# Twelve of sixteen tiles of h from seven half-size products, in two rounds that share their sums of a

## The chip, the cores and the metric

The kernel runs on one core of one Trainium2 chip. The metric is the device time of one execution in microseconds. A profile of one execution comes with it; its span, from the first to the last instruction, is somewhat shorter than the device time of the same run.

## The reference

```python
m, k, n, p = 1024, 1024, 2048, 1024
h = np.matmul(a, b)                     # a: 1024 x 1024, b: 1024 x 2048
h = 0.5 * h * (1 + np.tanh(np.sqrt(2 / np.pi) * (h + 0.044715 * h ** 3)))
return np.matmul(h, c).astype(np.float32)   # c: 2048 x 1024
```

All inputs and the output are float32 in HBM.

## The kernel before

The kernel computes h transposed. `hT[h]` holds, for one half h (0 or 1) of the 1024 rows of a, sixteen tiles t of 128 columns of h by 512 rows. A tile is a sum over eight k of a product of a 128x128 block of b (the stationary operand) with a 128x512 block of `aT`, the transposed a in bf16. A matmul of 512 columns is the unit of work on TensorE.

*Loads.* SyncE loads a and b in float32 into staging tiles, in pieces of 512 KB: four pieces of a (each one half h and 256 columns of k, a quarter q) and four of b (two k by 512 columns). VectorE or ScalarE casts them to bf16 (`cast_a`, `cast_b`). POOL issues the loads that cast on the way: the rest of a (`a2`), of b (`b1` for its first 1024 columns, `b2` for the others) and all of c (`c_sb`). They wait behind `gate`, a copy of one element on POOL that waits for SyncE's fifth piece. So SyncE's pieces have the DMA engines to themselves at first.

*Turns.* `turn1` and `turn` transpose eight 128x128 blocks of a on TensorE into PSUM; VectorE copies them to `aT`.

*The plain part.* Tiles 0 to 3 of both halves are accumulated over k 0 to 3 as the pieces arrive (`block`, `mm1`), and leave PSUM as float32 (`leave`, tile `half`). Tiles 4 to 7 follow over all eight k. Then tiles 0 to 3 get k 4 to 7 and are added to `half`. `gelu` on ScalarE writes `hT`. That is 128 matmuls (line L112).

*The rounds of seven products.* Tiles 8 to 15 come from a 2x2 block scheme with seven products in place of eight (class `Seven`, function `seven`). In order of issue `seven` calls them P1 (A11 B11), P2 (A12 B21), P5 (S1 T1), P6 (S2 T2), P7 (S3 T3), P3 (S4 B22) and P4 (-A22 T4). A is the quarter of b or of h, B that of a or of c. S1 to S4 and T1 to T4 are sums of quarters that VectorE forms in fp32r (`s1` to `s4`, `t1` to `t4`, line L199). `plain_s` and `plain_t` are ScalarE copies of A22 (negated) and of B22 into the same type. P1 and P2 read bf16, the other five fp32r. Product j of each kind makes one 128x512 tile; its matmuls are at line L241. P1, P6, P7 and P4 accumulate in the banks X (0 to 3), P2, P5 and P3 use the banks Y (4 to 7). After P1, P6 and P7 ScalarE takes snapshots of a bank (`snap`: p1, v and u, line L286). VectorE adds them to the Y banks (`plus`, line L291, tile `ot` with four buffers). Here `done` is `gelu` on the result. The object `one` makes tiles 8 to 15 this way (112 matmuls, k = 4 per product), and `two` the whole second product, h times c, into the output (216 matmuls of 512 columns and 16 of 256). The function `between` places the sums of a round, and the first sums of the next, between its products.

Each engine runs its instructions in the order in which the program writes them (`manual_schedule`). Where `seven` gives the end of a round, two of its parts that matter below are:

```python
        for j in range(4):
            done(1, 1, j, c22[j])
            w.product(py[j], w.last_s, w.t[3], j, False)
            done(0, 1, j, plus(py[j], v[j]))
        between("P3")
```

and, in `between1`, the sums of the second round t1, s1 and t2, in four pieces each, that VectorE forms from there on.

The large SBUF slots x0 to x3, a, b1 and b2 are used by one tile after the other: staging first, then `half` and the sums. A new tile in a slot waits for the last reader of the old one.

Of the kernel before, what the change touches and what calls it, by code (L numbers as in the profile page):

```python
# [19 lines left out]
def kernel(ctx, tc, a, b, c, out):  # L20
# [43 lines left out]
    stb = slot("x0", [128, 2, KH, H], F32, "stb")  # L64
    sta = slot("x1", [128, 2, 2, 4, 256], F32, "sta")

    def load_a(h, q):
        nc.sync.dma_start(out=sta[:, h, q], in_=av[:, 4 * h:4 * h + 4, ds(q * 256, 256)])  # L68

    def load_b(q, c):  # L70
        nc.sync.dma_start(out=stb[:, c, 2 * q:2 * q + 2], in_=bv[:, 2 * q:2 * q + 2, ts(c, H)])  # L71

    load_a(0, 0)
    load_b(0, 0)
    load_a(1, 0)
    load_a(0, 1)
    load_b(1, 0)
    load_a(1, 1)
    load_b(0, 1)
    load_b(1, 1)  # L80

    nc.gpsimd.tensor_copy(gate, stb[:, 0, 3, 0:1])
# [6 lines left out]
    a2 = {}  # L89
    for h in (0, 1):  # L90
        for m in (0, 2):
            st = pieces("m", 4, [128, 2, H], BF16, "a2")
            nc.gpsimd.dma_start(out=st, in_=av[:, 4 * h + m:4 * h + m + 2, ds(KH * 128, H)])
            a2[h, m] = st
    for k in range(KH, KT):
        nc.gpsimd.dma_start(out=b1[:, k], in_=bv[:, k, 0:1024])
# [13 lines left out]
    def mm1(p, t, h, ks, k0=0, k1=KT):  # L110
        for k in ks:
            nc.tensor.matmul(p, b1[:, k, ts(t, 128)], aT[:, h, k],  # L112
                             start=(k == k0), stop=(k == k1 - 1))
# [12 lines left out]
    def cast_a(h, q, eng):  # L126
        ab = pieces("ab", 2, [128, 4, 256], BF16, "ab")
        copy(eng, ab, sta[:, h, q])
        return ab

    def turn1(h, q, i, ab):
# [6 lines left out]
    def cast_b(k, c, n=1):  # L138
        for i in range(n):
            r = ds(i * (H // n), H // n)  # L140
            nc.scalar.activation(b1[:, k, ds(c * H + i * (H // n), H // n)], stb[:, c, k, r], AF.Copy)  # L141

    def block(h, tiles, ks):
        for k in ks:
            for t in tiles:
                mm1(ps[h, t], t, h, (k,), 0, KH)

    stir(7)
    turn1(0, 0, 4, cast_a(0, 0, nc.vector))
    stir(8)  # L150
    cast_b(0, 0, 2)
    cast_b(1, 0)
    block(0, range(4), (0, 1))
    turn1(1, 0, 5, cast_a(1, 0, nc.vector))
    for t in range(3):
        ps[1, t] = bank(4 + t)
    ab = cast_a(0, 1, nc.scalar)
    block(1, range(3), (0,))
    turn1(0, 1, 7, ab)
    block(1, range(3), (1,))  # L160
    cast_b(2, 0)
    cast_b(3, 0)
    ab = cast_a(1, 1, nc.vector)
    block(0, range(4), (2,))
    turn1(1, 1, 7, ab)
    block(0, range(4), (3,))
    for k in range(KH):
        cast_b(k, 1)
    half = slot("x3", [128, 2, 4, H], F32, "half")

    def leave(h, t):
        copy(nc.vector if t % 2 else nc.scalar, half[:, h, t], ps[h, t])


    for t in range(4):
        leave(0, t)
    block(1, range(3), (2, 3))
    ps[1, 3] = bank(7)
    mm1(ps[1, 3], 3, 1, range(KH), 0, KH)
    for t in range(4):  # L180
        leave(1, t)

    def turn(h, m, i):
        pt = bank(i, (128, KH, 256), BF16, "pt")
        for k in range(KH):
            for n in range(2):
                nc.tensor.transpose(pt[:, k, ts(n, 128)], a2[h, m][:, n, ts(k, 128)], ident)  # L187
        nc.vector.tensor_copy(aT[:, h, KH:KT, ds(m * 128, 256)], pt)


    class Seven:
        def __init__(self, kt, A, B, s, t):
            self.kt, self.A, self.B, self.s, self.t = kt, A, B, s, t
# [7 lines left out]
        def t1(self, n=1):  # L201
            self.dve(self.t[0], self.B[0][1], self.B[0][0], SUB, n)

        def t2(self, n=1):
            self.dve(self.t[1], self.B[1][1], self.t[0], SUB, n)

        def t3(self, n=1):
            self.dve(self.t[2], self.B[1][1], self.B[0][1], SUB, n)
# [18 lines left out]
        def plain_t(self, n=1):  # L227
            w = self.kt // n
            for i in range(n):
# [3 lines left out]
        def plain_s(self, n=1):  # L233
            w = self.kt // n
            for i in range(n):
# [3 lines left out]
        def product(self, p, l, r, j, start, c0=0, w=H):  # L239
            for k in range(self.kt):  # L240
# [4 lines left out]
    x = [slot(f"x{i}", [128, 2, 4, H], F32R, "x1") for i in range(3)]  # L245
    one = Seven(4, [[b2[:, 0:4, 0:H], b2[:, 4:8, 0:H]], [b2[:, 0:4, H:], b2[:, 4:8, H:]]],
                [[aT[:, 0, 0:4], aT[:, 1, 0:4]], [aT[:, 0, 4:8], aT[:, 1, 4:8]]],
                [x[i][:, 0] for i in range(3)] + [None], [x[i][:, 1] for i in range(3)] + [None])
    one.t1()


    T2 = [(h, t) for h in range(2) for t in range(4, 8)]
    for n, (h, t) in enumerate(T2[:7]):
        ps[h, t] = bank(n)
        mm1(ps[h, t], t, h, range(KH))
        if n in (2, 3, 4, 5):
            turn(n // 4, 2 * (n % 2), 7)
    one.t3()
    one.t2()
    for k in range(KH, KT):  # L260
        for h, t in T2[:4]:
            mm1(ps[h, t], t, h, (k,))
    for n, (h, t) in enumerate(T2[:7]):
        if n >= 4:
            mm1(ps[h, t], t, h, range(KH, KT))
# [171 lines left out]
```

## Time and profile before

| | |
|---|---|
| device time, three runs | 120.61, 120.62, 120.70 us |
| device time of the profiled run | 120.74 us |
| span of the profile | 119.0 us |
| TensorE, matmuls | 111.3 us busy, 94% |
| TensorE, weight loads | 72.6 us busy, 61% |
| VectorE | 88.5 us busy, 74% |
| ScalarE | 52.7 us busy, 44% |
| POOL | 14.6 us busy, 12% |
| granted TensorE clock | 1.0 |
| read from HBM, written | 20.97 MB, 4.19 MB |

By stage, from the busy times of each engine in each stretch:

| stretch, us | what | TensorE | VectorE | ScalarE |
|---|---|---|---|---|
| 0 to 14.2 | SyncE's loads, first blocks | 10.58 | 4.43 | 5.07 |
| 14.2 to 39.84 | plain part | 25.48 | 17.46 | 12.12 |
| 39.84 to 64.91 | first round (`one`) | 25.07 | 22.07 | 19.61 |
| 64.91 to 115.3 | second round (`two`) | 50.21 | 44.16 | 15.89 |

In the profile PE is TensorE's matmuls, PEld its weight loads, DVE is VectorE, ACT is ScalarE, POOL is GpSimd and SP is SyncE; SPq and POOLq are their issues of DMAs. A line such as "L241 PE MATMUL ps<-x,s ... x48" is a group of 48 matmuls from line 241 that read tiles x and s and write tile ps. In brackets stands the idle time ahead of an instruction and what ended it. Matmuls overlap in time, so the duration of one is longer than the distance between two starts.

### The profile page before, as it was taken

What the parts mean: (1) busy time and instruction counts of PE and PEld (TensorE: products, weight loads), DVE (VectorE), ACT (ScalarE), POOL (GpSimd) and SP (SyncE); (2) the same over time, 40 slices, a digit from 0 to 9 for tenths busy, and PEclk for the clock granted to TensorE, in tenths of its full rate; (3) what the DMA queues carried; (4) which work ended last, traced back from release to release, by engine and by line L of the source; (5) the groups of instructions that cost most, each with busy time, mean ns of one, the idle gap of its engine ahead of it and who ended that gap; (6) DMA issues with size and microseconds to landing.
All of it is one profiled execution on the core that took longest, in us unless ns stands there. A gap on an engine that the chain in (4) does not pass through costs nothing.

```text
span 119.0 us, 1467 instructions
## 1 busy us (share of the span) xinstructions
PE 111.3 (94%) x552; PEld 72.6 (61%) x558; DVE 88.5 (74%) x93; ACT 52.7 (44%) x86; POOL 14.6 (12%) x27
## 2 busy tenths in 40 slices
PE   5877999999999999999999999999999999999970
PEld 2424445554444445888887444488888888888850
DVE  0242689579048899797779999999999986944760
ACT  4045492005647789846679347800043982000000
POOL 2002985453222000000000000000000000000000
PEclk9999999999999999999999999999999999999999
DMA  2999999999999999995000000070000002024992
GB/s 89 280 364 374 347 204 212 170 206 205 207 209 211 213 211 210 212 211 107 4 3 0 6 0 0 0 264 0 0 0 0 6 0 88 0 90 178 357 354 79
DMA packets 11606, 16.86 MB, mean 142 GB/s; under 512 B 720, under 2 KB 6096, under 8 KB 11600
## 3 DMA queue, kind: packets, MB, share of 16 engines
q0 software_dynamic: 5952, 8.39, 39.9%
q1 hardware_dynamic: 5648, 8.39, 20.1%
q8 instruction: 4, 0.07, 0.2%
q14 instruction: 2, 0.02, 0.0%
HBM read 20.97 MB, written 4.19 MB: 212 GB/s over the span
## 4 chain that ended last, share of the span: by engine, by line
PE 85%; DMA 8%; SPq 2%; DVE 1%; issue 1%; DVEq 0%
PE ps L241 63%; PE ps L112 20%; DMA sta<-in_a_dram 8%; PE pt L187 2%; SPq L68 1%; SPq L71 1%; DVE ab L108 1%; PE pt L135 1%; DVE ot L342 0%; DVEq L108 0%
## 5 line engine op out<-in xcount | busy, mean ns | idle before, releaser
L112 PE MATMUL ps<-aT,b 128*128 128x512 bf16 x124 | 28.8, 379 | 2.0 <-ACT b L141 0.9
L241 PE MATMUL ps<-x,s 128*128 128x512 f32 x128 | 29.5, 390 | 0.0
L241 PEld LDWEIGHTS ps<-x,s 128*128 128x128 f32 x128 | 24.0, 188 | 5.1 <-DVE ot L291 0.2
L112 PEld LDWEIGHTS <-b 128*128 128x128 bf16 x128 | 12.1, 98 | 15.6 <-ACT b L141 1.5
L241 PE MATMUL ps<-x,x 128*128 128x512 f32 x64 | 14.8, 389 | 0.0
L241 PE MATMUL ps<-c_sb,hT 128*128 128x512 bf16 (+1 forms) x70 | 14.1, 355 | 0.1
L241 PEld LDWEIGHTS ps<-x,x 128*128 128x128 f32 x64 | 12.0, 188 | 2.5
L286 ACT ACTIVATE v<-ps 128x512 f32<-128x512 f32 x8 | 4.8, 599 | 15.4 <-PE ps L241 15.4
L241 PE MATMUL ps<-x 128*128 128x512 f32 x48 | 11.3, 393 | 0.0
L241 PEld LDWEIGHTS <-hT 128*128 128x128 bf16 x72 | 6.9, 98 | 7.1 <-issue 0.5
L116 ACT ACTIVATE hT<-ps 128x512 bf16<-128x512 f32 x12 | 6.3, 603 | 11.0 <-PE ps L112 11.0
L241 PEld LDWEIGHTS ps<-x 128*128 128x128 f32 x48 | 9.0, 188 | 2.0
L276 DVE TENSOR_TENSOR half<-ps,half 128x512 f32<-128x512 f32 x8 | 5.5, 692 | 5.5 <-PE ps L112 5.1
L199 DVE TENSOR_TENSOR x<-c_sb 128x1024 fp32r<-128x1024 bf16 x8 | 9.2, 1219 | 0.0
L291 DVE TENSOR_TENSOR ot<-ps,v 128x512 f32<-128x512 f32 x8 | 5.3, 687 | 4.6 <-DMA out_dram<-ot 3.8
L141 ACT ACTIVATE b<-stb 128x512 bf16<-128x512 f32 (+1 forms) x9 | 4.7, 573 | 6.6 <-DMA stb<-in_b_dram 6.6
L291 DVE TENSOR_TENSOR ot<-ps,u 128x512 f32<-128x512 f32 x8 | 5.4, 690 | 2.9 <-ACT u L286 2.9
L116 ACT ACTIVATE hT<-ot 128x512 bf16<-128x512 f32 x12 | 6.9, 624 | 1.1 <-DVE ot L291 1.1
L241 PE MATMUL ps<-aT,b 128*128 128x512 bf16 x32 | 7.1, 379 | 0.0
L102 POOL DMA_DIRECT2D c_sb<-in_c_dram x8 | 5.7, 712 | 10.3 <-DMA b<-in_b_dram 10.3
L116 ACT ACTIVATE hT<-half 128x512 bf16<-128x512 f32 x8 | 5.0, 630 | 2.6 <-DVE half L276 2.6
L108 DVE CAST ab<-sta 128x1024 bf16<-128x1024 f32 x3 | 2.1, 694 | 5.3 <-DMA sta<-in_a_dram 5.3
(49 smaller groups left out, 115.7 us busy)
## 6 DMA issues: line engine op xcount, KB each, us to landing
c_sb<-in_c_dram POOLq DMA_DIRECT2D x8, 512.0 KB, 20.6
out_dram<-ot SPq DMA_DIRECT2D x15, 256.0 KB, 2.1
sta<-in_a_dram SPq DMA_DIRECT2D x4, 512.0 KB, 7.0
stb<-in_b_dram SPq DMA_DIRECT2D x4, 512.0 KB, 9.1
b<-in_b_dram POOLq DMA_DIRECT2D x4, 512.0 KB, 13.9
a<-in_a_dram POOLq DMA_DIRECT2D x4, 256.0 KB, 5.8
b<-in_b_dram POOLq DMA_DIRECT2D x4, 256.0 KB, 9.1
out_dram<-ot SPq DMA_DIRECT2D x2, 128.0 KB, 2.0
```

Source lines behind the costliest of these rows:

```text
L68: nc.sync.dma_start(out=sta[:, h, q], in_=av[:, 4 * h:4 * h + 4, ds(q * 256, 256)])
L102: nc.gpsimd.dma_start(out=c_sb[:, t:t + 2], in_=cv[:, t:t + 2])
L108: nc.vector.tensor_copy(dst, src)
L112: nc.tensor.matmul(p, b1[:, k, ts(t, 128)], aT[:, h, k], start=(k == k0), stop=(k == k1 - 1))
L116: nc.scalar.activation(hT[h][:, t], p, AF.Gelu_apprx_tanh)
L141: nc.scalar.activation(b1[:, k, ds(c * H + i * (H // n), H // n)], stb[:, c, k, r], AF.Copy)
L187: nc.tensor.transpose(pt[:, k, ts(n, 128)], a2[h, m][:, n, ts(k, 128)], ident)
L199: nc.vector.tensor_tensor(out=dst[:, r], in0=x[:, r], in1=y[:, r], op=op)
L241: nc.tensor.matmul(p[:, ds(c0, w)], l[:, k, ts(j, 128)], r[:, k, ds(c0, w)], start=(start and k == 0), stop=(k == self.kt - 1), skip_group ...
L276: nc.vector.tensor_tensor(out=half[:, h, t], in0=p, in1=half[:, h, t], op=ADD)
L286: nc.scalar.activation(st, p, AF.Copy)
L291: nc.vector.tensor_tensor(out=ot, in0=p, in1=st, op=ADD)
```

## The change

- Tiles 4 to 7 no longer come from the plain part. A third object `zero` makes them from the second 512 columns of b in a small round of seven products, with quarters of 256 columns (n = 2 tiles per product), so 56 matmuls at k = 4. It runs ahead of `one` and issues P4 before P3. Its products use banks 0 and 1 (X), 2 and 3 (P2), and 4 and 5 (P5 and P3).
- The sums t1 to t4 of a and the copy of B22 are made once. `zero` and `one` share them. t1, t2, t3 and a half of the copy are made in the load phase, in pieces of two k, as the turned pieces of a arrive.
- Tiles 0 to 3 stay in PSUM over all eight k; `half`, its copies and its adds go.
- SyncE loads all of a (eight pieces) and the first 512 columns of b (four pieces): twelve pieces, 6 MB. POOL's `a2` loads go; its loads of b into `b1` are the second 512 columns for all eight k, in two pieces of 512 KB as written. `gate` waits for the tenth SyncE piece. All turns of a go through `cast_a`, on VectorE or ScalarE.
- In `one`, the negated copy of A22 is made in four pieces, one after each snapshot of P7, into the tile that held S2. s1 and s2 of `one` come after `zero`.
- In `two`, each store of a tile of the upper left quarter is split into two halves; where S3's slot is taken moves to a later line.

The parts of the diff that the text speaks of:

```diff
-    stb = slot("x0", [128, 2, KH, H], F32, "stb")
-    sta = slot("x1", [128, 2, 2, 4, 256], F32, "sta")
+    stb = slot("x0", [128, KT, H], F32, "stb")
+    sta = [slot(f"x{i}", [128, 2, 2, 4, 256], F32, "sta") for i in (1, 3)]
 
     def load_a(h, q):
-        nc.sync.dma_start(out=sta[:, h, q], in_=av[:, 4 * h:4 * h + 4, ds(q * 256, 256)])
-
-    def load_b(q, c):
-        nc.sync.dma_start(out=stb[:, c, 2 * q:2 * q + 2], in_=bv[:, 2 * q:2 * q + 2, ts(c, H)])
+        nc.sync.dma_start(out=sta[q // 2][:, h, q % 2],
+                          in_=av[:, 4 * h:4 * h + 4, ds(q * 256, 256)])
+
+    def load_b(q):
+        nc.sync.dma_start(out=stb[:, 2 * q:2 * q + 2], in_=bv[:, 2 * q:2 * q + 2, 0:H])
 
     load_a(0, 0)
-    load_b(0, 0)
+    load_b(0)
     load_a(1, 0)
-    load_a(0, 1)
-    load_b(1, 0)
-    load_a(1, 1)
-    load_b(0, 1)
-    load_b(1, 1)
-
-    nc.gpsimd.tensor_copy(gate, stb[:, 0, 3, 0:1])
+    for q in range(1, 4):
+        load_a(0, q)
+        load_b(q)
+        load_a(1, q)
+
+    nc.gpsimd.tensor_copy(gate, sta[1][:, 0, 1, 3, 0:1])
...
-    a2 = {}
-    for h in (0, 1):
-        for m in (0, 2):
-            st = pieces("m", 4, [128, 2, H], BF16, "a2")
-            nc.gpsimd.dma_start(out=st, in_=av[:, 4 * h + m:4 * h + m + 2, ds(KH * 128, H)])
-            a2[h, m] = st
-    for k in range(KH, KT):
-        nc.gpsimd.dma_start(out=b1[:, k], in_=bv[:, k, 0:1024])
+    for k in range(0, KT, 4):
+        nc.gpsimd.dma_start(out=b1[:, k:k + 4, H:], in_=bv[:, k:k + 4, ds(H, H)])
...
-    for k in range(KH):
-        cast_b(k, 1)
-    half = slot("x3", [128, 2, 4, H], F32, "half")
-
-    def leave(h, t):
-        copy(nc.vector if t % 2 else nc.scalar, half[:, h, t], ps[h, t])
-
-
-    for t in range(4):
-        leave(0, t)
-    block(1, range(3), (2, 3))
-    ps[1, 3] = bank(7)
-    mm1(ps[1, 3], 3, 1, range(KH), 0, KH)
-    for t in range(4):
...
-    def turn(h, m, i):
-        pt = bank(i, (128, KH, 256), BF16, "pt")
-        for k in range(KH):
-            for n in range(2):
-                nc.tensor.transpose(pt[:, k, ts(n, 128)], a2[h, m][:, n, ts(k, 128)], ident)
-        nc.vector.tensor_copy(aT[:, h, KH:KT, ds(m * 128, 256)], pt)
+                mm1(ps[h, t], t, h, (k,))
...
-    x = [slot(f"x{i}", [128, 2, 4, H], F32R, "x1") for i in range(3)]
-    one = Seven(4, [[b2[:, 0:4, 0:H], b2[:, 4:8, 0:H]], [b2[:, 0:4, H:], b2[:, 4:8, H:]]],
-                [[aT[:, 0, 0:4], aT[:, 1, 0:4]], [aT[:, 0, 4:8], aT[:, 1, 4:8]]],
-                [x[i][:, 0] for i in range(3)] + [None], [x[i][:, 1] for i in range(3)] + [None])
-    one.t1()
-
-
-    T2 = [(h, t) for h in range(2) for t in range(4, 8)]
-    for n, (h, t) in enumerate(T2[:7]):
-        ps[h, t] = bank(n)
-        mm1(ps[h, t], t, h, range(KH))
-        if n in (2, 3, 4, 5):
-            turn(n // 4, 2 * (n % 2), 7)
-    one.t3()
-    one.t2()
-    for k in range(KH, KT):
-        for h, t in T2[:4]:
-            mm1(ps[h, t], t, h, (k,))
-    for n, (h, t) in enumerate(T2[:7]):
-        if n >= 4:
-            mm1(ps[h, t], t, h, range(KH, KT))
-        gelu(t, h, ps[h, t])
-    p = bank(7)
-    mm1(p, 7, 1, range(KT))
-    gelu(7, 1, p)
-
-
-    for n in range(8):
-        h, t = divmod(n, 4)
-        p = bank(n)
-        mm1(p, t, h, range(KH, KT), KH)
-        nc.vector.tensor_tensor(out=half[:, h, t], in0=p, in1=half[:, h, t], op=ADD)
-        gelu(t, h, half[:, h, t])
-    x.append(slot("x3", [128, 2, 4, H], F32R, "x1"))
-    one.s[3], one.t[3] = x[3][:, 0], x[3][:, 1]
+    def pair(i):
+        x = slot(f"x{i}", [128, 2, 4, H], F32R, "x1")
+        return x[:, 0], x[:, 1]
+
+    BB = [[aT[:, 0, 0:4], aT[:, 1, 0:4]], [aT[:, 0, 4:8], aT[:, 1, 4:8]]]
+
+    def quarters(b, c0, w):
+        return [[b[:, 0:4, ds(c0, w)], b[:, 4:8, ds(c0, w)]],
+                [b[:, 0:4, ds(c0 + w, w)], b[:, 4:8, ds(c0 + w, w)]]]
+
+    zero = Seven(4, quarters(b1, H, 256), BB, [None] * 4, [None] * 4, 2)
+    one = Seven(4, quarters(b2, 0, H), BB, [None] * 4, zero.t)
+
+    stir(7)
+    turn(0, 0, 4, cast_a(0, 0, nc.vector))
+    stir(8)
+    cast_b(0, 2)
+    cast_b(1)
+    block(0, range(4), (0, 1))
+    turn(1, 0, 5, cast_a(1, 0, nc.vector))
+    for t in range(3):
+        ps[1, t] = bank(4 + t)
+    ab = cast_a(0, 1, nc.scalar)
+    block(1, range(3), (0,))
+    turn(0, 1, 7, ab)
+    block(1, range(3), (1,))
+    cast_b(2)
+    cast_b(3)
+    ab = cast_a(1, 1, nc.vector)
+    block(0, range(4), (2,))
+    turn(1, 1, 7, ab)
+    zero.t[0], zero.t[1] = pair(1)
+    zero.t1(2, 0)
+    block(0, range(4), (3,))
+    ab = cast_a(0, 2, nc.scalar)
+    cast_b(4)
+    cast_b(5)
+    block(1, range(3), (2,))
+    turn(0, 2, 7, ab)
+    block(1, range(3), (3,))
+    ab = cast_a(1, 2, nc.vector)
+    block(0, range(4), (4,))
+    turn(1, 2, 7, ab)
+    zero.t1(2, 1)
+    block(0, range(4), (5,))
+    ab = cast_a(0, 3, nc.scalar)
+    cast_b(6)
+    cast_b(7)
+    block(1, range(3), (4,))
+    turn(0, 3, 7, ab)
+    zero.t2(2, 0)
+    block(1, range(3), (5,))
+    ab = cast_a(1, 3, nc.scalar)
+    zero.t[3], x31 = pair(3)
+    zero.plain_t(2, 0)
+    block(0, range(4), (6,))
+    turn(1, 3, 7, ab)
+    zero.t[2], x21 = pair(2)
+    zero.t3(2, 0)
+    zero.t2(2, 1)
+    zero.t3(2, 1)
+    block(0, range(4), (7,))
+    for t in range(4):
+        gelu(t, 0, ps[0, t])
+    block(1, range(3), (6, 7))
+    for t in range(3):
+        gelu(t, 1, ps[1, t])
+    ps[1, 3] = bank(7)
+    mm1(ps[1, 3], 3, 1, range(KT))
+    gelu(3, 1, ps[1, 3])
+
+    t4, x01 = pair(0)
+    zero.s = [x31[:, :, 0:256], x01[:, :, 0:256], x21[:, :, 0:256], x01[:, :, 256:]]
+    one.s = [x31, x01, x21, x01]
...
-        px = [bank(i) for i in X]
+        J = range(w.n)
+        PX = X[:w.n]
+        P2, PY = (X[2:], Y[:2]) if w.n == 2 else (Y, Y)
+        px = [bank(i) for i in PX]
         p1, v, u = {}, {}, {}
...
-        for j in range(4 if w is one else 3):
-            p = bank(Y[j])
+        for j in J if w is not two else range(3):
+            p = bank(P2[j])
...
-        py = [bank(i) for i in Y]
+        py = [bank(i) for i in PY]
...
-        for j in range(4):
-            done(1, 1, j, c22[j])
-            w.product(py[j], w.last_s, w.t[3], j, False)
-            done(0, 1, j, plus(py[j], v[j]))
-        between("P3")
-        for j in range(4):
-            w.product(px[j], w.s[3], w.last_t, j, False)
-            done(1, 0, j, px[j])
+
+        def p3(first):
+            for j in J:
+                if first:
+                    done(1, 1, j, c22[j])
+                w.product(py[j], w.last_s, w.t[3], j, False)
+                done(0, 1, j, plus(py[j], v[j]))
+            between("P3")
+
+        def p4(first):
+            for j in J:
+                if first:
+                    done(1, 1, j, c22[j])
+                w.product(px[j], w.s[3], w.last_t, j, False)
+                done(1, 0, j, px[j])
+
+        for i, f in enumerate((p4, p3) if w.n == 2 else (p3, p4)):
+            f(i == 0)
         if w is two:
...
-    one.s1()
-    one.s2()
...
+    def done0(i, l, j, p):
+        gelu(4 + 2 * i + j, l, p)
+
+    def between0(n):
+        if n == "P1":
+            zero.plain_t(2, 1)
+        elif n == "P2":
+            zero.s3()
+            zero.plain_s()
+            zero.s4(x31[:, :, 256:])
+        elif n == "P5":
+            zero.t4(t4, 2)
+            one.last_t = t4
 
     def done1(i, l, j, p):
         gelu(8 + 4 * i + j, l, p)
 
     def between1(n):
-        if n == "P1":
-            one.plain_s()
-        elif n == "P2":
+        if n == "P2":
             one.s3()
-            one.plain_t()
         elif n == "P5":
             one.s4(one.s[0])
-            one.t4(one.t[0])
+        elif n[:2] == "P7":
+            one.plain_s(4, int(n[2]))
         elif n == "P3":
             two.t[0] = slot("x1", [128, 8, H], F32R, "x2")
             two.t1(4)
@@ -371,9 +383,15 @@
             two.t[1] = slot("x2", [128, 8, H], F32R, "x2")
             two.t2(4)
 
+    zero.s1()
+    zero.s2()
+    seven(zero, done0, between0)
+    one.s1()
+    one.s2()
     seven(one, done1, between1)
 
...
-        store(4 * i + j, l * H, H, p)
+        n = 2 if (i, l) == (0, 0) else 1
+        for q in range(n):
+            r = ds(q * (H // n), H // n)
+            store(4 * i + j, l * H + q * (H // n), H // n, p[:, r])
```

## The prediction

> **What bounds the kernel now.** I read the page's slices first, then the chain of waits, then TensorE's timeline by stage, then the timelines of the load phase and of the seam between the rounds. All sums are made against the profiled span of 119.0 us; its run took 120.74 us, the three others 120.61 to 120.70, so a change of the span is carried unchanged to the median of 120.62. About 0.2% (0.24 us) can be told from no change.
>
> From the page, the DMA share and the bytes moved, in slices of 3 us:
>
> ```profile
> DMA  2999999999999999995000000070000002024992
> GB/s 89 280 364 374 347 204 212 170 206 205 207 209 211 213 211 210 212 211 107 4 3 0 6 0 0 0 264 0 0 0 0 6 0 88 0 90 178 357 354 79
> ```
>
> Loads run without a gap to about 56 us, first SyncE's, then POOL's. The chain of waits (start, length, what):
>
> ```profile
> 13.54 0.62 PE pt L135 x8
> 14.16 5.69 PE ps L112 x26
> ...
> 40.00 25.30 PE ps L241 x113
> ```
>
> It hangs on the loads up to 13.5 us; from there to 115.24 us it is TensorE, nearly alone. So the change has to win TensorE time after the loads, or leave that start sooner. TensorE's timeline at the first round of seven products:
>
> ```profile
> 39.84 7.07 PE L241 MATMUL ps<-aT,b 128*128 128x512 bf16 x32
> 46.56 11.26 PE L241 MATMUL ps<-x 128*128 128x512 f32 x48
> 57.65 7.42 PE L241 MATMUL ps<-x,x 128*128 128x512 f32 x32
> 64.91 12.26 PE L241 MATMUL ps<-c_sb,hT 128*128 128x512 bf16 x54
> ```
>
> Starts, not durations, give the prices. 57.65 to 64.91 is 32 fp32r products: 0.2269 us each. The round takes 64.91 - 39.84 = 25.07 us; less 80 x 0.2269 = 18.15, 6.92 are left for 32 bf16 products: 0.2163 each. Check on the second round: 56 x 0.2163 + 160 x 0.2269 = 48.41; its first 256-wide matmul starts at 113.30, 48.39 later. Neither round waits anywhere.
>
> **What the skill says.** "TensorE: Matmul & The Clock Gate", section "Wait — 56ns, not 53.3ns?", gives 215.7 ns from start to start for 512 columns when warm; the bf16 figure agrees, the fp32r one is 11 ns above it. "ScalarE: Activation LUTs", "What ACT_TABLE_LOAD costs", gives 186 ns + 0.833 ns per element, with some 93 ns of overlap: 0.52 us per step at 512. The eight 128x512 copies at L231 take 4.26 us, 0.53 each. "DMA: Bandwidth & Descriptors", "Issuing engines are not separate DMA queues", says that all issuers share the same 16 engines; the slices agree, POOL's bytes follow SyncE's.
>
> **TensorE's work.** Of 464 matmuls of 512 columns, h took 128 plain + 112. It will take 64 plain + 56 (seven products of 2 tiles x 4 k) + 112: eight fewer. But 40 of the 56 read fp32r sums, at 0.0106 more each. Net gain 8 x 0.2163 - 40 x 0.0106 = 1.73 - 0.42 = 1.3 us, if TensorE starts equally early. The 64 transposes stay. It does not start equally early, since loads now pace 64 plain matmuls in place of 32.
>
> **The load phase.** The timeline, with the idle time ahead in brackets:
>
> ```profile
> 11.28 0.18 POOL L82 COPY gate<-stb 128x1 f32<-128x1 f32 x1 [9.97 <-DMA stb<-in_b_dram]
> ...
> 15.38 1.15 ACT L141 ACTIVATE b<-stb 128x512 bf16<-128x512 f32 x2 [0.17 <-DMA stb<-in_b_dram]
> ...
> 16.79 0.75 POOL L99 DMA_DIRECT2D b<-in_b_dram  x1 [0.25 <-DMA a<-in_a_dram]
> ```
>
> SyncE's second load landed at 6.66 us (the first cast of b starts at 6.71) and the eighth at 15.33: 1.445 us per 512 KB. Four more give 21.1; gaps that end in a piece of a averaged 1.59 (1.46, 1.76, 1.54), which gives 21.7. I take 21.2 for the last piece of a. Its cast on ScalarE takes 1.06, its eight transposes 0.45, with 0.1 of handovers: the last turn ends at T = 22.8. Could TensorE itself be later? From 13.99, where the same fourth turn ended before, it has 28 matmuls (6.06) and three turns (1.35), and waits for copies of a turned piece (0.69 each on VectorE) for some 0.8: ready at 22.2. So the load decides, and T lies between 22.65 (TensorE) and 23.6 (a later last piece, from sharing with POOL).
>
> From T come 18 plain matmuls and 16 bf16 products (34 x 0.2163 = 7.35) and 40 fp32r ones (9.08), plus 0.08 for the copy of the last turned piece: the big round starts at T + 16.5 = 39.3. Before, from 13.99: 110 x 0.2163 + four turns at 0.53 = 25.9, giving 39.84. Gain 0.54 us, with T's bounds +0.7 to -0.25. So most of the 1.3 us is eaten by the later start.
>
> **What else leaves and comes.** The eight copies to half, eight adds on VectorE (0.69) and the casts of b's second 512 columns leave; TensorE waited for none of them after 14 us, so they return nothing. Four more casts of a come (three on ScalarE, one on VectorE), six half sums of aT move into VectorE's load-phase queue (1.22 alone, 1.14 back to back), four sums for the small round come, and one copy on ScalarE. The sums t1 to t4 and the copy of B22 are made once, in the small round, and leave the big one, where nothing waited for them. In VectorE's order the last turned piece is copied by 23.7, three half sums follow to 27.1, then s1 and s2, which need both POOL loads of b.
>
> POOL's gate moves from the fifth load to the tenth, 15.33 + 2 x 1.445 = 18.2. Behind it on POOL stand all casting loads, 2 MB of a fewer than before. Before, the first landed 5.5 us after the gate (11.28 to 16.75) and each 512 KB cost 2.53 (issues of c at 31.55, 34.09, 36.70). So b's columns 512 to 1023 land at 25.0 and 27.6 at the latest. The same skill page's section "Anatomy of one DMA — SWDGE (gpsimd) path" gives 2.0 us + bytes/436 GB/s, an estimate of 4.4 us for 1 MB, thus 22.7 and 25.1 at the earliest. I take the late ends. P1 needs the first at 26.7: fine. s1, s2, two adds, s3, s4 and t4 in two pieces end at 27.6 + 6 x 1.14 + 1.4 = 35.9. Product P4 needs t4's second piece at T + 13.3 = 36.1. Slack 0.2. The last c lands near 27.6 + 12 x 2.53 = 58, before its first use at 62.5. With two tiles, a snapshot must end within 5 x 0.2269 = 1.13 of the last matmul of its tile; before, the one at 51.51 took 0.39 + 0.05 + 0.60 + 0.05 = 1.09. It fits by 0.04. I charge 0.1 for the small round, bounds 0 and 1.0. The three stores in halves add three issues on SyncE near 77 us, with no store queued ahead: nothing.
>
> **The seam.** The big round's copy of -A22 moves from after P1 into P7, as four pieces of 0.53 on ScalarE between the snapshots. There ScalarE is not idle enough:
>
> ```profile
> 57.91 0.60 ACT L286 ACTIVATE u<-ps 128x512 f32<-128x512 f32 x1 [0.31 <-PE ps L241]
> ...
> 60.53 2.08 DVE L291 TENSOR_TENSOR ot<-ps,v 128x512 f32<-128x512 f32 x3 [0.70 <-ACT hT L116]
> 61.25 2.72 ACT L116 ACTIVATE hT<-ot 128x512 bf16<-128x512 f32 x5 [0.24 <-DVE ot L291]
> 62.53 4.62 DVE L199 TENSOR_TENSOR x<-c_sb 128x1024 fp32r<-128x1024 bf16 x4
> 63.88 2.03 ACT L116 ACTIVATE hT<-ps 128x512 bf16<-128x512 f32 x4
> ```
>
> Between snapshots it idled 0.31 three times. Four pieces of 0.53 less 0.31 x 3 and some overlap make the last snapshot 0.39 late and the first gelu after it 0.92 late (58.41 to 59.33). VectorE's adds wait for those gelus (the 0.70), the gelus for the adds, so nothing is caught up: the gelu that frees bank 0 ends at 65.27 in place of 64.45, where the second round wants that bank at 64.91: 0.4 us. VectorE leaves its last add 0.83 late, and then has 13.6 us of sums without a gap, to an add at 76.15 that frees the bank of product P5, which starts at 76.89:
>
> ```profile
> 76.15 1.88 DVE L291 TENSOR_TENSOR ot<-ps,p 128x512 f32<-128x512 f32 x3
> ...
> 76.89 22.07 PE L241 MATMUL ps<-x,s 128*128 128x512 f32 x96
> ```
>
> No slack there either, so the 0.83 reaches TensorE in full (the 0.4 is part of it). Bounds: 0, if the adds do not follow the gelus, and 1.1. Later waits have over 1 us. The end after the last matmul is the same code.
>
> **Sum.** -0.54 + 0.1 + 0.83 = +0.4: 121.0 us. The likeliest case's own range is 120.6 to 121.5.
>
> **Rivals.** (1) The forecast, 43%. (2) The seam has slack: gelus and adds catch up before 64.9 us, because the first gelus of the seam have their input ready and ScalarE steps at 0.53. It decides where ScalarE's lateness is under 0.46 (64.91 - 64.45) and VectorE's is made good. For it: before, ScalarE idled 0.84 ahead of the gelu at 59.87. Against it: the 0.70 wait of the adds. Then -0.54 + 0.1: 120.2, and 120.0 with T at its early end; 32%. (3) The small round starves: POOL's loads or the half sums put s1 past 27.6. Each microsecond beyond delays product P4 by one; a landing 1 us later with the seam gives 122.0; 15%. (4) The load phase itself is slower, a piece of a landing at 22.5 and casts queued behind each other: T = 24.2, 122.4; 10%. That the products are not fewer can be excluded: the loops count them.
>
> **Chances.** Faster: most of (2), 0.30. Same: (1)'s lower part and a little of (2), 0.17. Slower: the rest of (1), (3), (4), 0.53. The range 120.0 to 122.4 leaves out 2 in 10.
>
> **What would show it.** The last turn ends near 22.8, the big round starts near 39.3, and ScalarE's first gelu of the seam comes about 0.9 us later after the last P7 product than now, with TensorE waiting for ScalarE at the second round's start and for VectorE at its product P5. No such waits: rival 2. A wait of VectorE for a POOL load near 27 us, or of product P4 for t4: rival 3. It would be wrong in kind if waits inside the big round decided.

## The result, and the profile after

The changed kernel takes 122.10 us (median of four runs, 121.99 to 122.45) against 120.66 (120.61 to 120.75) for the kernel before on the same chip: ratio 1.0124, 95% interval 1.0106 to 1.0141. The span of its profile is 120.4 us (before: 119.0). The change makes the kernel 1.4 us slower; the forecast was 0.4 us slower.

The page's DMA share and bytes moved, in slices of 3 us:

```profile
DMA  3999999999999999997000000043000002004993
GB/s 97 274 375 361 365 355 275 197 206 207 207 207 211 211 213 212 210 211 148 3 0 0 5 0 0 0 147 115 0 0 0 0 5 87 0 8 181 363 357 137
```

SyncE's fast stretch is now six slices long in place of four, and POOL's slow one (about 210 GB/s) follows. These figures count what is written: POOL's loads read float32 and write bf16, so they read twice as much. Line numbers moved: L193, L106, L277, L282 and L110 are now what L241, L112, L286, L291 and L116 were before. The chain of waits:

```profile
12.13 10.50 DMA sta<-in_a_dram
...
22.73 1.06 ACT ab L100
...
24.46 3.96 PE ps L106 x18
28.43 27.86 PE ps L193 x124
...
78.79 38.34 PE ps L193 x176
```

It hangs on the last piece of a up to 22.6 us, where it left the loads at 13.5 before. Between 56.28 and 78.79 us it runs over ScalarE and VectorE, where it was TensorE alone before. TensorE's timeline at the stage starts (24.30 is the T of the prediction, the first matmul after the last turn):

```profile
24.30 4.13 PE L106 MATMUL ps<-aT,b 128*128 128x512 bf16 x18
...
41.00 7.08 PE L193 MATMUL ps<-aT,b 128*128 128x512 bf16 x32
...
66.41 12.25 PE L193 MATMUL ps<-c_sb,hT 128*128 128x512 bf16 x56 [0.17 <-ACT hT L110]
78.79 22.05 PE L193 MATMUL ps<-x,s 128*128 128x512 f32 x96
```

Against the starts of before (39.84 for the first round, 64.91 for the second, 76.89 for P5), TensorE is 1.16 us later at the big round, 1.50 at the second round and 1.90 at P5. So 1.16 us arise ahead of the big round and 0.74 at the seam. Only 1.4 arrive in the span: from the end of VectorE's last add to the end of the span it takes 2.8 us, before 3.3. In the load phase:

```profile
18.45 0.18 POOL L82 COPY gate<-sta 128x1 f32<-128x1 f32 x1 [17.14 <-DMA sta<-in_a_dram]
...
21.39 1.15 ACT L135 ACTIVATE b<-stb 128x512 bf16<-128x512 f32 x2 [1.83 <-DMA stb<-in_b_dram]
...
22.73 1.06 ACT L100 ACTIVATE ab<-sta 128x1024 bf16<-128x1024 f32 x1 [0.20 <-DMA sta<-in_a_dram]
```

The tenth piece opens the gate at 18.45. The eleventh and twelfth land just before 21.4 and 22.7, where 1.445 us per piece from there gives 19.8 and 21.3. And at the seam:

```profile
57.38 0.59 ACT L277 ACTIVATE u<-ps 128x512 f32<-128x512 f32 x1
...
60.37 0.65 ACT L110 ACTIVATE hT<-ot 128x512 bf16<-128x512 f32 x1
...
62.44 2.08 DVE L282 TENSOR_TENSOR ot<-ps,v 128x512 f32<-128x512 f32 x3 [0.70 <-ACT hT L110]
...
65.79 0.57 ACT L110 ACTIVATE hT<-ps 128x512 bf16<-128x512 f32 x1
```

From the second on, the snapshots of u no longer have an idle time in brackets: copies stand between them. The gelu that frees bank 0 for the second round runs to 66.36, and TensorE starts at 66.41.

### The profile page after: what moved, and what is told of

Same layout as the page of the kernel before. It is cut to its first block, busy times and chain, and to the rows that moved or that the text cites. A ratio compares the mean times of both kernels' runs of the same rounds, so it can differ in the third digit from the quotient of the medians.

```text
span 120.4 us, 1483 instructions
## 1 busy us (share of the span) xinstructions
PE 112.5 (93%) x550; PEld 76.0 (63%) x550; DVE 90.1 (75%) x96; ACT 57.9 (48%) x96; POOL 11.0 (9%) x21
## 4 chain that ended last, share of the span: by engine, by line
PE 59%; DVE 10%; SPq 9%; DMA 9%; issue 5%; ACT 5%; ACTq 0%; DVEq 0%
PE ps L193 55%; DMA sta<-in_a_dram 9%; SPq L68 5%; DVE s L151 4%; DVE x L151 4%; SPq L72 4%; PE ps L106 3%; DVE ot L282 2%; ACT u L277 2%; ACT hT L110 1%; ACT x L189 1%; ACT ab L100 1%; PE pt L129 1%; DVE ot L346 0%; ACTq L100 0%
## 5 line engine op out<-in xcount | busy, mean ns | idle before, releaser
L193 PE MATMUL ps<-x,s 128*128 128x512 f32 x128 | 29.5, 390 | 0.1
L193 PEld LDWEIGHTS ps<-x,s 128*128 128x128 f32 x128 | 24.0, 188 | 5.6 <-DVE ot L282 0.6
L193 PE MATMUL ps<-x,x 128*128 128x512 f32 x80 | 19.1, 394 | 0.0
L106 PE MATMUL ps<-aT,b 128*128 128x512 bf16 x64 | 15.9, 379 | 2.4 <-ACT b L135 1.4
L193 PEld LDWEIGHTS ps<-x,x 128*128 128x128 f32 x80 | 15.0, 188 | 3.3
L193 PE MATMUL ps<-x 128*128 128x512 f32 x72 | 16.8, 391 | 0.0
L193 PEld LDWEIGHTS ps<-x 128*128 128x128 f32 x72 | 13.2, 188 | 3.3 <-ACT v L277 0.2
L277 ACT ACTIVATE v<-ps 128x512 f32<-128x512 f32 x10 | 6.0, 598 | 18.3 <-PE ps L193 18.3
L193 PE MATMUL ps<-c_sb,hT 128*128 128x512 bf16 (+1 forms) x72 | 14.2, 355 | 0.2 <-ACT hT L110 0.2
L110 ACT ACTIVATE hT<-ot 128x512 bf16<-128x512 f32 x18 | 10.8, 627 | 4.3 <-DVE ot L282 4.2
L282 DVE TENSOR_TENSOR ot<-ps,v 128x512 f32<-128x512 f32 x10 | 6.7, 688 | 6.7 <-DMA out_dram<-ot 3.9
L106 PEld LDWEIGHTS <-b 128*128 128x128 bf16 x64 | 5.8, 97 | 9.3 <-ACT b L135 2.5
L193 PEld LDWEIGHTS <-hT 128*128 128x128 bf16 x72 | 7.0, 98 | 7.3 <-issue 0.8
L130 DVE COPY aT<-pt 128x1024 bf16<-128x1024 bf16 x8 | 5.5, 692 | 7.3 <-PE pt L129 7.3
L282 DVE TENSOR_TENSOR ot<-ps,u 128x512 f32<-128x512 f32 x10 | 6.8, 691 | 5.7 <-ACT u L277 5.7
L193 PE MATMUL ps<-aT,b 128*128 128x512 bf16 x48 | 10.7, 379 | 0.0
L193 PEld LDWEIGHTS <-b 128*128 128x128 bf16 x48 | 4.6, 98 | 5.7 <-issue 0.3
L110 ACT ACTIVATE hT<-ps 128x512 bf16<-128x512 f32 x14 | 7.3, 601 | 0.1
L277 ACT ACTIVATE p<-ps 128x512 f32<-128x512 f32 x9 | 5.3, 595 | 3.9 <-PE ps L193 3.9
L100 ACT ACTIVATE ab<-sta 128x1024 bf16<-128x1024 f32 x4 | 4.2, 1057 | 5.9 <-DMA sta<-in_a_dram 4.0
## 6 DMA issues: line engine op xcount, KB each, us to landing
c_sb<-in_c_dram POOLq DMA_DIRECT2D x8, 512.0 KB, 19.8
```

Of the source, the lines that this page charges most:

```text
L100: nc.scalar.activation(dst, src, AF.Copy)
L106: nc.tensor.matmul(p, b1[:, k, ts(t, 128)], aT[:, h, k], start=(k == 0), stop=(k == KT - 1))
L110: nc.scalar.activation(hT[h][:, t], p, AF.Gelu_apprx_tanh)
L130: nc.vector.tensor_copy(aT[:, h, 2 * q:2 * q + 2], pt)
L193: nc.tensor.matmul(p[:, ds(c0, w)], l[:, k, ts(j, 128)], r[:, k, ds(c0, w)], start=(start and k == 0), stop=(k == self.kt - 1), skip_group ...
L277: nc.scalar.activation(st, p, AF.Copy)
```

## The experiments

The theory at first: the last piece of a lands late because POOL's loads share the DMA engines with it from the gate on (e1, e2), and the copies of -A22 inside P7 cost the seam (e3). Each experiment is on the changed kernel if nothing else is said; the ratios are to the kernel before.

**e1, the gate one piece later.**

```diff
-    nc.gpsimd.tensor_copy(gate, sta[1][:, 0, 1, 3, 0:1])
+    nc.gpsimd.tensor_copy(gate, stb[:, 7, 0:1])
```

> Theory (POOL's loads, let go at the tenth SyncE piece, share the DMA engines with the last two pieces and hold them up by 1.5 us): with the gate on the eleventh piece, that piece lands at 19.7 instead of 21.34 us and the last piece of a at 21.0 to 21.3 instead of 22.7; the first matmul after the last turn starts at 22.6 to 22.9 instead of 24.30, b's second columns land at 25.2 and 27.8 or sooner, the big round starts at 39.3 to 39.6 instead of 41.00, and the run takes 120.4 to 120.8 us instead of 122.1. Rival (twelve pieces in a row are slower by themselves, by SyncE's issues): the last piece still lands at 22.5 or later, the small round then waits for b, and the run takes 122.0 or more.

Measured: 122.01 us, ratio 1.0111 (1.0091 to 1.0130). The eleventh piece lands at 19.9, but the last one hardly earlier than in the changed kernel:

```profile
22.56 1.06 ACT L100 ACTIVATE ab<-sta 128x1024 bf16<-128x1024 f32 x1 [1.49 <-DMA sta<-in_a_dram]
```

ScalarE stood idle for 1.49 us ahead of it. Sharing with POOL, now let go after the eleventh piece, does not explain the last one.

**e2, nothing shares at all:** the gate waits for the last piece.

```diff
-    nc.gpsimd.tensor_copy(gate, sta[1][:, 0, 1, 3, 0:1])
+    nc.gpsimd.tensor_copy(gate, sta[1][:, 1, 1, 3, 0:1])
```

> Theory: with the gate on the last piece nothing shares with SyncE; the last piece lands at 20.9 to 21.2 us and the turn ends at 22.6. But POOL's first bytes move 2 us after the gate, so b's second columns land at about 26.6 and 29.1: s1 waits for them, product P4 of the small round waits some 1.5 us for t4, the big round starts at about 40.7, the run takes 121.7 us. Rival (SyncE's own issues): last piece at 22.5, b at 31, the run takes 123.5 or more.

Measured: 123.74 us, ratio 1.0250 (1.0228 to 1.0273). With no load of POOL's before it, the last piece still lands at 22.5. The DMA view of 20.6 to 22.6 us, in slices of 0.05 us:

```profile
DMA  0010201010000001000000010000000000000000
...
DMA packets 32, 0.03 MB, mean 15 GB/s; under 512 B 3, under 2 KB 32, under 8 KB 32
...
q1 hardware_dynamic: 32, 0.03, 5.5%
```

Almost every engine is idle. What is left of the last piece is 32 packets, whose times fill 5.5% of sixteen engines, nine tenths of one. "DMA: Bandwidth & Descriptors" in the Trainium skill, section "Why a DMA increments its semaphore by 16 and not by 1", says that a transfer runs on up to 16 engines which finish independently, and that all of its data has landed only when all have reported. The view agrees. So do the sixteen completion signals of each load, whose times the traces keep, without the engine's name and outside the views shown here: of the last piece in e2, fifteen come between 20.41 and 21.38 us and one at 22.48. In the changed kernel it is fifteen by 21.14 and one at 22.62; of its eleventh piece, fifteen by 19.75 and one at 21.36; of its tenth, all by 18.39. So one engine is late, and everyone waits for it. Something had held that engine up before 20.6 us.

The late gate itself costs 1.7 us more than e1: b's second columns come too late, and the small round starves for them at P2. The bracket of P2's matmuls names the snapshot p, but the loads of their weights wait 1.13 us for the DMA of b, up to 30.70, and s1 on VectorE, which needs no snapshot, starts at 30.94 after 2.49 us of idling; what both need is POOL's second piece of b. This is the prediction's rival of a starving small round, made on purpose:

```profile
30.71 1.90 PE L193 MATMUL ps<-aT,b 128*128 128x512 bf16 x8 [0.64 <-ACT p L277]
```

**e3, the seam without the copies on ScalarE:** one copy on VectorE, after P6.

```diff
-        elif n[:2] == "P7":
-            one.plain_s(4, int(n[2]))
+        elif n == "P6":
+            nc.vector.tensor_scalar_mul(one.s[3], b2[:, 4:8, H:], -1.0)
```

> Theory (the four copies of -A22 between ScalarE's snapshots delay the gelus and adds of the seam by 0.9 us and cost 0.74): with that copy as one instruction on VectorE after P6, where VectorE idles 2.9 us, the second round starts 25.07 us after the big one instead of 25.41, its product P5 11.98 us later instead of 12.38, and the run takes 121.35 us. The load phase stays as it is. Rival (the waits at the seam come from s1 and s2 of the big round, now behind the small one on VectorE): the two distances stay at 25.4 and 12.4, the run at 122.1.

Measured: 121.17 us, ratio 1.0039 (1.0023 to 1.0054), so 0.93 less than the changed kernel. Lines of its timelines, VectorE's first, then TensorE's:

```profile
55.10 1.23 DVE L377 TENSOR_SCALAR x<-b 128x2048 fp32r<-128x2048 bf16 x1 [1.33 <-PE ps L193]
...
65.78 12.26 PE L193 MATMUL ps<-c_sb,hT 128*128 128x512 bf16 x56
77.76 4.61 PE L193 MATMUL ps<-x,s 128*128 128x512 f32 x19
```

The big round starts at 40.70 there, so it is 25.08 us to the second round and 11.98 from there to P5: to 0.01 us what the kernel before needs, and no waits in brackets. The copy lies in a gap of VectorE's, between its sums and the adds of P7: in the changed kernel VectorE idled there for 2.93 us. The seam's 0.74 us are those four copies, shown by their removal. The rest of the 0.93 lies ahead of the big round, which this edit does not touch (T is 23.96 here, 24.08 to 24.30 in the changed kernel, e1, e2 and e8: scatter).

**e4, both:** e3 with the gate of e1.

> Theory: the two costs are in different places and add up: 1.4 us from the gate and 0.74 from the seam give 119.8 to 120.1 us, faster than the kernel before at 120.66. Rival (the seam's waits are hidden or shifted when the load phase shortens): no more than the better of the two alone, 120.5 or more.

Measured: 121.25 us, ratio 1.0044 (1.0029 to 1.0059), the same as e3; the last piece lands at 22.5 again. A clear miss. With e1, e2 and e4 the theory of sharing is dead, for a gate at the tenth piece or later.

**What held the engine up.** The page's list of DMA queues shows a third queue, "q8 instruction", with four packets of 16 KB in the whole run. The DMA view finds the first of the changed kernel between 19.1 and 19.2 us, amid the last pieces (window 18.8 to 20.6):

```profile
q1 hardware_dynamic: 469, 0.48, 79.8%
...
q8 instruction: 1, 0.02, 3.9%
```

3.9% of 16 engines over 1.8 us is 1.12 us on one engine. In the kernel before, the same packet starts between 20.5 and 20.6, after SyncE's last piece (15.3); there, it met only loads of POOL's. "Runtime: NRT & Kernel Launch" in the skill, section "Instruction fetch mechanics", says that an engine's sequencer fetches its instructions in blocks of 16 KiB, 256 instructions, over a DMA queue of its own, and calls the cost "mostly hidden". The size agrees. In each of before, after, e3 and e10 the packet comes when 215 matmuls and weight loads of TensorE are on record (some are missing from a trace), and in the kernel before the next three packets come after 214, 233 and 251 more. So it follows TensorE's count of instructions, if not to the instruction (see e5). Hidden it is not: TensorE does not wait for it, but a transfer spread over all engines does.

The new theory: the fetch keeps one engine for about 1.1 us, this engine's share of the last piece lands that much late, and the place of the fetch moves with the number of TensorE instructions ahead of it. Its tests need no change of any load. (The expectations of these runs give the starts of fetches some 0.25 us higher, counted from another zero.)

**e5, the fetch later:** e3 with the 15 narrow warm-up matmuls between the first turns as two wide ones, 26 TensorE instructions fewer.

```diff
-    stir(7)
+    nc.tensor.matmul(ps[0, 3], warm[:, 0:128], warm, start=True, stop=True, skip_group_check=True)
     turn(0, 0, 4, cast_a(0, 0, nc.vector))
-    stir(8)
+    nc.tensor.matmul(ps[0, 3], warm[:, 0:128], warm, start=True, stop=True, skip_group_check=True)
```

> The kernel of e3 with the fifteen small warm-up matmuls as two wide ones: 26 instructions fewer on TensorE ahead of the load phase. Theory (TensorE fetches 16 KB of instructions when it is at about its 217th instruction; that packet holds one DMA engine for 1.15 us at 19.4 us, and since each piece is spread over all engines, the last piece of a lands 1.15 us late): the fetch moves to about 21.2 us, behind SyncE's last bytes, the last piece lands at 21.2 to 21.4 instead of 22.35 us, the last turn is followed by the first matmul at 22.8 to 23.0 instead of 23.96, and the run takes 119.9 to 120.3 us instead of 121.17. Rival (the twelfth piece in a row is slow for a reason of its own, SyncE's queue or its descriptors): it still lands at 22.3 to 22.5, and the run takes 121.2 us.

Measured: 120.08 us, ratio 0.9962 (0.9939 to 0.9985), 1.09 us less than e3. The fetch starts between 20.4 and 20.5, and the last piece is there a microsecond earlier. Its cast in e3, then in e5:

```profile
22.39 1.06 ACT L100 ACTIVATE ab<-sta 128x1024 bf16<-128x1024 f32 x1 [1.62 <-DMA sta<-in_a_dram]
...
21.46 1.06 ACT L100 ACTIVATE ab<-sta 128x1024 bf16<-128x1024 f32 x1 [0.36 <-DMA sta<-in_a_dram]
```

The profiled execution was one of the longer ones of this kernel (121.05 us): its first matmuls of 512 columns ran slowly, eight of them from 7.27 to 10.58 us, and TensorE itself, not the load, was late at T (23.89). Four of this kernel's 17 executions took 120.88 us or more, so fewer warm-up matmuls seem to have a price of their own in some; e10 takes that away. The fetch was expected half a microsecond later, behind SyncE's last bytes, and it came with only 186 matmuls and weight loads on record. So the count of executed instructions does not fix it when TensorE is late; that TensorE's sequencer had read further ahead is a guess.

**e6, the fetch earlier:** e3 with 20 narrow matmuls in place of 8, 24 instructions more.

```diff
-    stir(8)
+    stir(20)
```

> The kernel of e3 with twelve more small warm-up matmuls, in a stretch in which TensorE waits anyhow: 24 instructions more. Theory: the fetch moves from 19.35 to about 17.7 us; now the tenth and the eleventh piece are late as well (19.3 and 20.7 us instead of 18.3 and 19.6), and the twelfth lands at 22.4 as before, since the engine that fetched stays behind. Rival (the twelfth piece is slow for a reason of its own): the tenth and eleventh land at 18.3 and 19.6, the twelfth at 22.4.

Measured: 121.21 us in one run; the fetch starts between 17.3 and 17.4. ScalarE's casts of the tenth and of the twelfth piece:

```profile
19.79 1.06 ACT L100 ACTIVATE ab<-sta 128x1024 bf16<-128x1024 f32 x1 [3.26 <-DMA sta<-in_a_dram]
...
22.54 1.06 ACT L100 ACTIVATE ab<-sta 128x1024 bf16<-128x1024 f32 x1 [0.34 <-DMA sta<-in_a_dram]
```

Now the tenth piece is late already (19.7; 18.3 in e3), so are the eleventh (21.0; 19.6 in e3) and the twelfth (22.4). Of the sixteen signals of each of the three, one alone is late, by 1.3 us after the others. An engine that has once fallen behind stays behind to the last piece. This fits a queue per engine that is worked in order; it does not fit a disturbance of one moment.

**e7, much sharing:** the gate back at the fifth piece of the new order, where POOL's loads run beside seven pieces of SyncE's.

```diff
-    nc.gpsimd.tensor_copy(gate, sta[1][:, 0, 1, 3, 0:1])
+    nc.gpsimd.tensor_copy(gate, stb[:, 3, 0:1])
```

> The changed kernel with the gate on the fifth piece, where the kernel before had it. Theory (sharing with POOL's loads is cheap as long as little is left to SyncE, as the gates at the tenth to twelfth piece showed, but costs what POOL moves when seven pieces are left): from about 14 us on both queues move, SyncE's last piece lands at 26 to 29 us instead of 22.7, the first matmul after the last turn comes at 28 to 31 us, and the run takes 126 to 129 us. Rival (SyncE's pieces keep the engines to themselves until they are done): the last piece lands at 22.7, and b's second columns earlier than now, the run takes 121.9 us.

Measured: 131.40 us in one run, worse than expected. The last piece lands at 29.3, T is 31.28: 6.98 later than in the changed kernel. The other 2.3 us are not explained; TensorE's granted clock is at half for some 10 us from 25.6 us on, and whether the idling caused that was not tried.

**e8, whole stores:** the stores in halves undone.

```diff
-        n = 2 if (i, l) == (0, 0) else 1
+        n = 1
```

> The changed kernel with whole stores of the upper left quarter. From the last matmul to the end of the span it took 0.48 us less than the kernel before, and e1 to e3 did so too. Theory (the halves change the order in which the last stores and waits fall): with whole stores the run takes 0.4 to 0.5 us more, 122.55. Rival (it comes from elsewhere): no change, 122.1 us.

Measured: 122.12 us, ratio 1.0116 (1.0083 to 1.0149), the changed kernel's time. A miss: the halves of the stores as such are not worth 0.4 to 0.5 us. Its loads are those of the changed kernel, line for line, and here the eleventh piece lands at 19.9 and the twelfth at 22.4. So whether the fetch catches the eleventh piece too, as in the changed kernel's profile (21.4), differs between executions; the last piece is late either way.

**e9, the end, in the kernel before.** In the traces, SyncE's last waits are for eight DMA semaphores in turn, and its DMAs take these semaphores in rotation. Of 25 DMAs (before) the last one takes the first semaphore, and seven waits follow; of 32 (after) it takes the last one, and none follows; of 29 (e8), three. Stores in halves in the kernel before bring its DMAs from 25 to 32, with nothing else changed:

```diff
-        store(4 * i + j, l * H, H, p)
+        n = 2 if i == l else 1
+        for q in range(n):
+            r = ds(q * (H // n), H // n)
+            store(4 * i + j, l * H + q * (H // n), H // n, p[:, r])
```

> The kernel before, with seven stores of the second round in halves, so that SyncE issues 32 DMAs in place of 25. Theory (at the end SyncE waits for eight DMA semaphores in turn, 0 to 7, and the DMAs take them in rotation; the last of 25 DMAs sits on the first of them, so seven further waits of some 0.07 us come after it, the last of 32 on the last one): the stretch from the last data to the end falls from 1.90 to 1.42 us, and the run takes 120.15 to 120.25 us instead of 120.65. Rival (the shorter end of the changed kernel comes from something else, the load phase or POOL's fewer loads): no change, 120.65 us.

Measured: 120.14 us (119.84 to 120.26), ratio 0.9955 (0.9939 to 0.9971). SyncE's wait for its stores, in total, number and longest, before and in e9:

```profile
SPq L432 <- DMA out_dram<-ot: 1.5, 1, 1.5
```

```profile
SPq L435 <- DMA out_dram<-ot: 1.1, 3, 0.5
```

In the kernel before, SyncE sits on the first semaphore for 1.5 us and then goes through the seven others, 0.06 us each; in e9 the waits end one by one while data still lands. The chain's last add ends at 115.68 in before and at 115.58 in e9, but the span ends at 119.0 and 118.4. From the last landing to the end it is 1.32 and 0.89 us. This was forecast from the rotation and found in another kernel. e8 fits in its trace: with three waits behind the last landing this stretch is 1.07 us, 0.17 more than the changed kernel's 0.89. That is too little for its four runs (122.05 to 122.27) to show, and less than half of what e8 had been expected to cost.

**e10, e3 with both warm-ups as two wide matmuls each,** 22 TensorE instructions fewer than e3, with more warm-up than e5.

```diff
-    stir(7)
+    for _ in range(2):
+        nc.tensor.matmul(ps[0, 3], warm[:, 0:128], warm, start=True, stop=True, skip_group_check=True)
     turn(0, 0, 4, cast_a(0, 0, nc.vector))
-    stir(8)
+    for _ in range(2):
+        nc.tensor.matmul(ps[0, 3], warm[:, 0:128], warm, start=True, stop=True, skip_group_check=True)
```

> The kernel of e3 with the fifteen small warm-up matmuls as four wide ones (22 instructions fewer), two in each place, to keep TensorE as busy as the small ones did[...]. Theory: the fetch comes at about 20.5 us, when most engines are done with SyncE's pieces; the last piece of a lands at 21.2 to 21.5 us, the first matmul after the last turn starts at 22.9 to 23.1, and the run takes 119.9 to 120.1 us, also in the profiled run. Rival (at 20.5 us the engine that fetches still has SyncE's packets): the last piece lands at 22.0 or later, and the run takes 120.7 to 121.2 us.

Measured: 120.08 us (120.02 to 120.15), ratio 0.9953 (0.9941 to 0.9966). The fetch in the DMA view of 20.4 to 20.5 us, ScalarE's cast of the last piece and TensorE's T:

```profile
q8 instruction: 1, 0.02, 70.8%
...
21.30 1.06 ACT L100 ACTIVATE ab<-sta 128x1024 bf16<-128x1024 f32 x1 [0.35 <-DMA sta<-in_a_dram]
...
22.87 4.13 PE L106 MATMUL ps<-aT,b 128*128 128x512 bf16 x18
```

All sixteen signals of the last piece come by 21.20: no engine is late. The first eight matmuls of 512 columns take from 7.14 to 8.94 us, so the slow start of e5's profile is not there. T is 1.09 us earlier than in e3, and the time is less by as much (121.17 - 120.08 = 1.09; the kernel before took 120.63 beside e3 and 120.59 beside e10). This version is faster than both kernels, than the kernel before by half a per cent.

## Why the prediction was near, and where it failed

The time lies in the range and on the side given the most chance, but 1.1 us above the forecast; what came is nearest to rival 4 in its numbers (a landing at 22.5, T = 24.2, 122.4), not in its cause. That it is no further off is in part luck: a cost of 1.5 us in the load phase and a gain of 0.47 at the end were both missed, and they have opposite signs.

- **TensorE's work: right.** e3 gives 25.08 and 11.98 us for the big round and for the second round up to P5; the prices 0.2163 and 0.2269 hold for the shared sums too. From T to the big round the sum gave 16.5 plus 0.1 for waits; measured 16.70 (weight loads wait 0.2 for v and 0.2 for u, where the working saw 0.04 us of room).
- **The load phase: the step that failed.** Last piece of a expected at 21.2, measured 22.6; T expected at 22.8 within 22.65 to 23.6, measured 24.30, outside its bounds. Casts (1.06), turns (0.46) and TensorE's own readiness (22.14 in e10, expected 22.2) were right. What was missing is a term that is not in the kernel's text: TensorE's instruction fetch, about 1.1 us of one DMA engine at 19.2 us. With the fetch out of the way (e10) the last piece lands at 21.2 and T is 22.87, the forecast's values. The late bound named sharing with POOL as its cause, and e1, e2 and e4 refute that for a gate at the tenth piece or later. The trace of before had the fetch in its list of queues; its start, set against TensorE's count of instructions, would have put it into SyncE's twelve pieces.
- **The gate and b's second columns: right in substance.** The gate opened at 18.45 (expected 18.2). P4 did not wait for t4, nor s1 for b; s1 started at 28.51 behind VectorE's half sums. Rival 3 came only when forced (e2).
- **The seam: right in mechanism and size.** Expected 0.83 with 0.4 of it at bank 0; measured 0.74 with 0.34 (25.41 against 25.07 us) and 0.40 (12.38 against 11.98) at P5. TensorE waited for ScalarE first and for VectorE then, as forecast:

```profile
78.06 1.88 DVE L282 TENSOR_TENSOR ot<-ps,p 128x512 f32<-128x512 f32 x3
...
78.79 1.23 PEld L193 LDWEIGHTS ps<-x,s 128*128 128x128 f32 x6 [0.63 <-DVE ot L282]
```

  The weights for P5 are loaded only when the first of these adds has freed its bank (78.75). Rival 2 is refuted by these waits.
- **"The end after the last matmul is the same code": wrong by about 0.47 us, in the kernel's favour.** The code is the same, but seven more DMAs of SyncE (four loads, three halves of stores) moved the last store to another place in the rotation of semaphores. e9 shows this for the kernel before: 0.45 us for the same number of DMAs. I had priced the halves at nothing.

The sum: +1.16 ahead of the big round (-0.54 forecast, +1.50 from T, +0.2 from the small round) + 0.74 - 0.47 = +1.43, measured +1.44.

What the scheme itself is worth, without the two costs that do not belong to it: in e10's profile the big round starts 0.25 us earlier than before, and the rest of its advantage is the end, which e9 gives to the kernel before as well. Measured side by side, e10 and e9 have medians of 120.08 and 120.14 us, with overlapping intervals: no difference that these runs can tell. Eight matmuls fewer are 1.3 us of TensorE, and waiting for twelve pieces of loads in place of eight takes most of it.

What stays open: that one engine of sixteen is late is shown by the signals; that it is the one which moved the fetch is inferred from the times (in e5, e6 and e10 the fetch moved, and the late pieces with it), since the traces name the engine neither of a packet nor of a signal.

## What to carry to other kernels

A load phase is not only the loads that the kernel issues: find the instruction queue's packets in the DMA view, set them against TensorE's count of instructions, and see whether one falls among the pieces on which the start of the work depends; removing a few instructions can move it off (here 22). A copy that is handed to an engine with short gaps between snapshots costs what exceeds the gaps, and the chain of adds and gelus behind it passes this on in full; look for one long gap on another engine. Before crediting a gain to a new scheme, give the old kernel the side effects too, here the number of DMAs.

## What was not expected of the hardware

- One packet of instructions, 16 KB, takes 0.9 to 1.2 us of a DMA engine in the kernels before and after, and its effect on a spread transfer lasts until SyncE's last piece (e6: three pieces, each 1.2 to 1.4 us late).
- Where the last DMA falls in the rotation of eight semaphores is worth 0.45 us at the end (e9), about 0.06 us for each wait that follows (0.43 over seven in the trace of before).
- Loads that cast look slow only by the bytes written. In e7, between 20 and 25 us, POOL's write 0.54 MB and SyncE's 0.79 MB, 268 GB/s together, where SyncE alone moves about 360. But POOL's read twice what they write: counted as read, it is 1.87 MB, or 374 GB/s. So the bytes that POOL reads are enough to account for the late plain pieces of e7; a further cost of mixing the two kinds is not shown.
- A copy with a change of sign on VectorE, 128x2048 from bf16 to fp32r, takes 1.23 us; ScalarE needs four steps of some 0.63.
